# Encoder layer on one core: the value products of a head are issued one query tile later, and the read-back of its deviations is postponed

## The chip, the cores and the metric

The program runs on one core of a Trainium2 chip. The metric is device time in microseconds (us). TensorE (PE) does the matrix products, VectorE (DVE) and ScalarE (ACT) read the results out of the accumulators, GpSimd (POOL) helps, and SyncE (SP) issues almost all transfers. Each engine works through its own instructions in the order of the program; semaphores make one wait for another.

## The reference, cut to what matters

Two request groups of 1024 rows pass through one encoder layer with shared weights:

```python
proj = x @ w_in                          # x: layer norm of the input
s = einsum('bqhcd,bkhcd->bhcqk', q, k) * scale      # 4 heads, 2 maps (c) each
p = softmax(s); a = p[:, :, 0] - lam * p[:, :, 1]
o = einsum('bhqk,bkhd->bqhd', a, v)                 # "value products"
o_da = rms_norm(o, subln_g) * (1 - lam_init) * silu(g)
o_mx = cross-attention of 4 heads into 256 memory rows, times silu(g)
o_cv = gated width-3 convolution
x = layer_norm(alpha * x + concat(o_da, o_cv, o_mx) @ w_o)
```

Everything is float32. Each large product is done as three products of a high and a low half (hi x hi, hi x lo, lo x hi).

## The kernel before

The attention is cut into 20 jobs, numbered 0 to 19 here: for each group, the four heads with two halves of 512 query rows each, then two memory jobs (numbers 8, 9, 18 and 19). A job has four tiles. In tile s, `score` issues the scores of 128 query rows against all keys (12 matmuls into two accumulator tiles `ps` of the pool `psS`, which has two buffers), then the two row maxima `mx` on DVE (L633), two exponentials `e` on ACT (L634), and, when the planner's clock says so, the combination of the two maps on DVE (L639 to L642). `turn` (L677) transposes two key blocks of the job before into a `pt`, which takes a buffer of the same pool `psS`; ACT copies it to `th` (L690), and DVE makes the low half `tl` (L155). `av` (L695) issues the six value products into the accumulator `po` (its third product of a block, L714, reads `tl`; in memory jobs there are four products, L707 and L708). After the fourth `av` of a head, `end_head` squares `po` on ACT (L737) and multiplies it by gain and gate on DVE (L739, output `og`).

Between these steps stand the "passes": three matmuls each (L389 to L391) of the projection tiles, later of the output projection (L872). A projection tile of 512 columns takes 8 passes. `job_steps` writes a job as 20 steps, five to a tile, and `run` issues the job's passes in equal shares after each step. Before, the five steps of a tile are: scores; nothing; `turn` of the job before; nothing; `av` of the job before. So there are two shares of passes from scores to `turn`, two from `turn` to `av`, and one from `av` to the next scores. A written plan gives each job its passes: 48 for jobs 1, 2, 4, 13 and 15, 64 for 3 and 5, 56 for 6, 40 for 7, 8, 9, 16 and 17, and 32 for 0, 10, 11, 12, 14, 18 and 19. After job 19 a last loop runs its `turn` and `av` between passes of the output projection.

A planner's clock `fl.t` (ns) counts TensorE work only: 650 for a pass, 1400 for scores, 880 for a `turn`, 1380 for an `av`. `after(ns, fn)` emits `fn` into the engine's program that much later on this clock. A list `extra` holds small steps on TensorE with due times, which `run_extra` emits after passes: the turning of value tiles (accumulator `pvt`), the sum of a head's squares (`rms`, accumulator `pr`, L745) and the turning of its deviations (`rows`, accumulator `pw`). All three use the one buffer of `psX`. After `rows`, the deviations `rw` are written to DRAM (`rd`), read back spread over the partitions (`rb`, L768), and multiplied into `og` on POOL (`fin`, L771), which is then stored.

Buffers that matter: `sq`, `rw`, `rb` and the memory jobs' `bot` share one buffer (tag "sq"); `og` has two, `th` and `tl` one each, `po` one, "ev" (projection read-outs and loads) five. In jobs 7 and 8 `norm_rows` normalises the second group's input: loads `xt`, DVE (L291), POOL (L295, L152), DVE (L155).

Of the kernel before, what the change touches and what calls it, by code (L numbers as in the profile page):

```python
# [27 lines left out]
F32 = mybir.dt.float32  # L28
F32R = mybir.dt.float32r
AF = mybir.ActivationFunctionType  # L30
ALU = mybir.AluOpType
# [4 lines left out]
P = 128  # L36
D = 1024
S = 1024
HS = 512
KB = D // P  # L40
H = 4
DH = 64
# [23 lines left out]
FD = 800  # L66
RD = 2500
MD = 800

SETS = (("Q", 4), ("K", 4), ("V", 4), ("G", 4), ("CB", 2), ("CC", 2), ("CH", 2), ("CG", 2),  # L70
        ("QM", 2), ("GM", 2), ("MK", 2), ("MV", 2))
# [23 lines left out]
class Flow:  # L95
# [10 lines left out]
    def after(self, ns, fn):  # L106

        done = []

        def once():  # L110
            if not done:
                done.append(True)
                fn()
        self.n += 1
        heapq.heappush(self.due, (self.t + ns, self.n, once))
        return once
# [8 lines left out]
def encoder(ctx, tc, x0, x1, xt0, xt1, memt, wt, wo, cols, lam4, rope, ln_rows, y0, y1):  # L125
    nc = tc.nc
    X, XT, Y = (x0, x1), (xt0, xt1), (y0, y1)
    fl = Flow()
    after = fl.after
# [11 lines left out]
    def sb(shape, dt, tag, name):  # L141
        return pool.tile(shape, dt, tag=tag, name=name, bufs=BUFS.get(tag, 1))

    def bank(shape, name):

        return psX.tile(shape, F32, tag="x", name=name)

    dma = nc.sync.dma_start
    V, G, A, T = nc.vector, nc.gpsimd, nc.scalar, nc.tensor
# [4 lines left out]
    def lo_of(out, x, hi, eng=None):  # L154
        (eng or V).tensor_tensor(out, x, hi.bitcast(F32), op=ALU.subtract)  # L155
# [97 lines left out]
    def keep_stats(g):  # L253

        def turn():
            pw = bank([16, P], "pst")
            T.transpose(pw, stats[g].rearrange("p i t -> p (i t)"), const["ident"])
            rw = sb([16, P], F32, "sq", "strw")
            A.activation(rw, pw, AF.Copy)
            fl.pe(110)  # L260
            after(800, lambda: dma(st_d[g].rearrange("i (t c) -> (i t) c", c=P), rw))
        extra.append((fl.t, turn))
# [149 lines left out]
    def store(dst, src, ns=1500):  # L412
        after(ns, lambda: dma(dst, src))
# [147 lines left out]
    EVAC = dict(Q=evac_q, K=evac_k, V=evac_v, G=evac_gate(g_d), CB=evac_cb, CC=evac_cc, CH=evac_ch,  # L561
                CG=evac_cg, QM=evac_qm, GM=evac_gate(gm_d), MK=evac_mk, MV=evac_mv)

    extra = []

    def run_extra():

        while extra:
            due = min(extra, key=lambda x: x[0])
            if due[0] > fl.t:  # L570
                return
            extra.remove(due)
            due[1]()


    class Job:
# [70 lines left out]
        def score_mem(self, qt):  # L647
# [18 lines left out]
            def norm(h):  # L666
                if h == 0:
                    V.reciprocal(r, sm)  # L668
                s = slice(h * NMEM, (h + 1) * NMEM)
                G.tensor_scalar(e[:, s], e[:, s], r[:, h:h + 1], 1.0, op0=ALU.mult, op1=ALU.mult)  # L670
            for h in range(H):
                self.late.append(after(3000 + MD * h, lambda h=h: norm(h)))
            self.tiles.append(e)
# [3 lines left out]
        def turn(self, s):  # L677
            while self.late:
                self.late.pop(0)()
            b = 2 * (MEMORDER[s] if self.mem else s)  # L680
            pt = psS.tile([P, S], F32, tag="s", name="pt")
            for u in range(2):
                for i in range(4):
                    T.transpose(pt[:, u * HS + i * P:u * HS + (i + 1) * P],  # L684
                                self.tiles[i][:, (b + u) * P:(b + u + 1) * P], const["ident"])
            th = sb([P, S], F32R, "th", "th")
            tl = sb([P, S], F32R, "tl", "tl")

            def halves():
                A.activation(th, pt, AF.Copy)  # L690
                self.t = th, tl, after(1200, lambda: lo_of(tl, pt, th))
            self.t = th, tl, after(400, halves)
            fl.pe(880)

# [25 lines left out]

        def end_mem(self, h):
            po, p, r0 = self.po, h // 2, (h % 2) * DH
            bot = sb([DH, HS], F32, "sq", "bot")
            A.activation(bot, po[DH:P, :], AF.Copy)
            if h % 2 == 0:
                self.og = sb([P, HS], F32, "og", "ogm")
            og = self.og
            V.tensor_tensor(og[r0:r0 + DH, :], po[0:DH, :], bot, op=ALU.add)
            if h % 2 == 1:
                gt = self.gt[p]  # L730
                V.scalar_tensor_tensor(og, og, 0.5, gt, op0=ALU.mult, op1=ALU.mult)
                store(mix_d[self.g][self.half][6 + p], og)
# [9 lines left out]
        def rms(self):  # L742
            pr = bank([P, 4], "pr")
            for i in range(4):
                T.matmul(pr[:, i:i + 1], self.sq[:, i * P:(i + 1) * P], const["ones"], start=True, stop=True)  # L745
            ms, r0 = sb([P, 4], F32, "small", "ms"), self.r0
            V.scalar_tensor_tensor(ms, pr, 1.0 / P, r0, op0=ALU.mult, op1=ALU.mult)
            rs = sb([P, 4], F32, "small", "rs")
            G.tensor_tensor(ms, ms, r0, op=ALU.mult)
            G.tensor_scalar(ms, ms, 1.0, EPS, op0=ALU.mult, op1=ALU.add)  # L750
            G.tensor_tensor(ms, ms, const["mhalf"][:, 0:4], op=ALU.pow)
            G.tensor_tensor(rs, ms, r0, op=ALU.mult)
            g, h, half, og = self.g, self.h, self.half, self.og
            rd = dram.tile([4, P], F32, name=f"rd{g}_{h}_{half}")

            def rows():

                pw = bank([4, P], "pw")
                T.transpose(pw, rs, const["ident"])
                rw = sb([4, P], F32, "sq", "rw")  # L760
                V.tensor_copy(rw, pw)
                fl.pe(110)
                after(1500, lambda: dma(rd, rw))
                after(5000, lambda: spread())

                def spread():
                    self.rb = sb([P, HS], F32, "sq", "rb")
                    dma(self.rb, flat(rd, 0, [[0, P], [1, HS]]))  # L768

                def fin():  # L770
                    G.tensor_tensor(og, og, self.rb, op=ALU.mult)  # L771
                    store(mix_d[g][half][h], og)
                after(9500, fin)
            extra.append((fl.t + 6000, rows))
            fl.pe(100)

    def job_steps(job, prev, nxt):

        out = []
        memory = nxt and nxt.mem and not job.mem  # L780
        for s in range(4):
            out.append([lambda s=s: job.score(s)])
            out.append([])
            if prev:
                out.append([lambda s=s: prev.turn(s)])
                out.append([])
                out.append([lambda s=s: prev.av(s)])
            if prev and s == (0 if prev.mem else 1):
                out[-1].append(prev.load_gates)
            if s == 1:  # L790
                if memory:
                    out[-1].append(nxt.load_memory)
            if s == 2 and memory:
                out[-1].append(nxt.split_memory)
            if s == 3 and nxt and nxt.mem and job.mem:
                out[-1].append(lambda: (setattr(nxt, "k", job.k), setattr(nxt, "v", job.v)))
        return out

    def run(steps, until):

        total = fillers.left() - sum(KB for it in fillers.items[until:] if it[0] != "do")
        done = 0
        for n, step in enumerate(steps):
            for fn in step:
                fn()
            while done < total * (n + 1) // len(steps):
                fillers.step()
                done += 1
                run_extra()
# [115 lines left out]
    until = []  # L925
# [39 lines left out]
    jobs = [Job(g, h, half) for g in range(2) for h in (0, 1, 2, 3, None) for half in range(2)]  # L965
# [41 lines left out]
    while fillers.i < n_first:  # L1007
        fillers.step()
        run_extra()
        while early and early[0][0] <= fl.t:  # L1010
            early.pop(0)[1]()
    prev = None
    for n, job in enumerate(jobs):
        if n == 19:
            load_wo(0, W0)
        if n < 2:
            for i in range(4):
                after(1000 + 8000 * i, lambda t=4 * n + i: stats_step(t))
        if n in (7, 8):
            new_hT(n - 7)  # L1020
            norm_rows(1, n - 7, 3300, *(("cu", "cy") if n == 8 else ("cy", "cu")), (X1, X2, X3))
        run(job_steps(job, prev, jobs[n + 1] if n + 1 < len(jobs) else None), until[n])
        prev = job
    for s in range(4):
        if s == 0:
            prev.load_gates()
        prev.turn(s)
        for k in range(6):
            fillers.step()
            run_extra()  # L1030
        prev.av(s)
        for k in range(3):
            fillers.step()
            run_extra()
    while not fillers.done():
        fillers.step()
    fl.flush()
# [32 lines left out]
```

## Time and profile before

| | us |
|---|---|
| median of 3 runs (1322.15 to 1327.23) | 1324.88 |
| the profiled execution | 1324.38 |
| its span, first to last instruction | 1322.6 |
| PE busy | 1204.0 (91%) |
| DVE busy | 874.6 (66%) |
| POOL busy | 466.3 (35%) |
| ACT busy | 426.4 (32%) |

The mean granted TensorE clock is 0.969 of full speed. A matmul's busy time overlaps that of the next one, so PE's busy share is read together with its waits: 100% busy means only that no gap is longer than the overlap.

### The profile page before, as it was taken

Reading aid. Unit: us, or ns where it says so; the run is one execution under the profiler, and the core shown is the slowest. Engines: PE = TensorE matmul, PEld = TensorE weight load, DVE = VectorE, ACT = ScalarE, POOL = GpSimd, SP = SyncE. Lnnn points to the kernel's source line nnn. Section 1 sums busy time; section 2 is a strip of 40 time slices with the busy share of each in tenths; the row PEclk is TensorE's granted clock in tenths of the full one; section 3 lists DMA queues with packets and bytes.
Section 4 is the critical chain, followed back from the end, with each engine's and each line's share of the span. In section 5 each row is a group of like instructions: output and inputs, shape, how many; then the busy total and the mean of one; then the engine's idle time right before and its main releaser. Section 6 shows DMA issues by size and latency. Waiting matters only on the chain.

```text
span 1322.6 us, 15444 instructions
## 1 busy us (share of the span) xinstructions
PE 1204.0 (91%) x5850; PEld 930.8 (70%) x5850; DVE 874.6 (66%) x1211; ACT 426.4 (32%) x707; POOL 466.3 (35%) x500
## 2 busy tenths in 40 slices
PE   6779799999999997779988989999999999899997
PEld 4557567777777785657756667767777777688886
DVE  5688856574566567774766666656656657787776
ACT  3333233233323243233433332432323344221110
POOL 4544411141033325484511113313312236544443
PEclk8889999999999998988999999999999999899999
DMA  7514122111111333332301011021122136635441
GB/s 282 183 41 136 48 72 72 49 56 48 56 57 32 96 115 125 104 97 78 113 24 48 17 57 43 30 79 50 33 72 72 33 126 208 207 121 174 143 143 48
DMA packets 62138, 118.64 MB, mean 90 GB/s; under 512 B 5264, under 2 KB 23920, under 8 KB 61936
## 3 DMA queue, kind: packets, MB, share of 16 engines
q1 hardware_dynamic: 58608, 111.36, 25.4%
q10 hardware_dynamic: 3456, 6.29, 1.2%
q8 instruction: 46, 0.75, 0.2%
q14 instruction: 28, 0.23, 0.1%
HBM read 93.47 MB, written 24.17 MB: 89 GB/s over the span
## 4 chain that ended last, share of the span: by engine, by line
PE 56%; DVE 20%; ACT 7%; POOL 7%; issue 5%; DMA 3%; SPq 1%; POOLq 0%; DVEq 0%; ACTq 0%
PE pout L872 10%; PE ps L626 7%; ACT e L634 4%; DVE tl L155 3%; DVE mx L633 3%; PE po L714 3%; PE pt L684 3%; DVE e L642 2%; PE pV L389 2%; PE pV L390 2%; PE pV L391 2%; PE po L713 2%; PE po L712 2%; DVE wl L155 1%; PE pQ L389 1%
## 5 line engine op out<-in xcount | busy, mean ns | idle before, releaser
L634 ACT ACTIVATE e<-ps,mx 128x1024 f32<-128x1024 f32 x128 | 142.9, 1116 | 345.4 <-DVE mx L633 345.4
L633 DVE TENSOR_REDUCE mx<-ps 128x1 f32<-128x1024 f32 x128 | 150.6, 1218 | 94.7 <-PE ps L626 94.5
L152 POOL TENSOR_SCALAR wh<-wraw 128x1024 fp32r<-128x1024 f32 (+1 forms) x73 | 76.2, 1044 | 245.6 <-PE pCC L390 54.6
L155 DVE TENSOR_TENSOR wl<-wraw,wh 128x1024 fp32r<-128x1024 f32 (+1 forms) x72 | 95.6, 1328 | 32.1 <-POOL wh L152 25.3
L155 DVE TENSOR_TENSOR tl<-pt,th 128x1024 fp32r<-128x1024 f32 x80 | 97.4, 1217 | 11.5 <-ACT th L690 11.0
L872 PE MATMUL pout<-woh,mixh 128*128 128x512 f32 x256 | 101.9, 398 | 0.0
L872 PE MATMUL pout<-woh,mixl 128*128 128x512 f32 x256 | 101.1, 395 | 0.1
L872 PE MATMUL pout<-wol,mixh 128*128 128x512 f32 x256 | 100.4, 392 | 0.0
L690 ACT ACTIVATE th<-pt 128x1024 fp32r<-128x1024 f32 x80 | 82.1, 1027 | 50.6 <-PE pt L684 49.9
L714 PE MATMUL po<-tl,vh 128*128 128x512 f32 x128 | 56.6, 442 | 42.8 <-DVE tl L155 42.4
L642 DVE SCALAR_TENSOR_TENSOR e<-e,ssum,e 128x1024 f32<-128x1024 f32 x64 | 89.1, 1392 | 0.0
L427 POOL TENSOR_TENSOR sw<-sw,ropet 128x512 f32<-128x512 f32 x32 | 41.8, 1306 | 115.0 <-DVE sw L421 115.0
L864 POOL TENSOR_TENSOR xr<-xr,lnrow 128x512 f32<-128x512 f32 x32 | 54.5, 1721 | 67.4 <-DVE xr L861 67.4
L684 PE MATMUL pt<-ident,e 128*128 128x128 f32 x512 | 68.9, 279 | 8.3 <-ACT e L634 8.2
L684 PEld LDWEIGHTS pt<-ident,e 128*128 128x128 f32 x512 | 60.2, 144 | 21.0 <-ACT e L634 14.6
L714 PEld LDWEIGHTS po<-tl,vh 128*128 128x128 f32 x128 | 25.2, 197 | 62.0 <-DVE tl L155 57.3
L626 PE MATMUL ps<-kh,qh 64*128 64x512 f32 x256 | 58.1, 450 | 0.0
L389 PE MATMUL pK<-hTh,wh 128*128 128x512 f32 x128 | 53.4, 417 | 4.6 <-ACT hTh L299 3.2
L872 PEld LDWEIGHTS pout<-woh,mixl 128*128 128x128 f32 x256 | 48.5, 189 | 11.7 <-DVE mixl L155 0.5
L872 PEld LDWEIGHTS pout<-wol,mixh 128*128 128x128 f32 x256 | 48.5, 190 | 10.6
L872 PEld LDWEIGHTS pout<-woh,mixh 128*128 128x128 f32 x256 | 48.6, 190 | 9.9
L670 POOL TENSOR_SCALAR em<-em,rm 128x256 f32<-128x256 f32 x64 | 35.8, 571 | 54.7 <-DVE rm L668 50.5
(227 smaller groups left out, 3121.9 us busy)
## 6 DMA issues: line engine op xcount, KB each, us to landing
wraw<-in_wt SPq DMA_DIRECT2D x73, 512.0 KB, 3.6
mraw<-mix SPq DMA_DIRECT2D x16, 512.0 KB, 6.2
xr<-in_x SPq DMA_DIRECT2D x16, 512.0 KB, 6.1
out<-xr ACTq DMA_DIRECT2D x24, 256.0 KB, 2.0
x<-in_x SPq DMA_DIRECT2D x8, 512.0 KB, 9.1
gate<-gs SPq DMA_DIRECT2D x16, 256.0 KB, 2.1
xs<-in_x SPq DMA_DIRECT2D x8, 512.0 KB, 5.8
gt<-gate SPq DMA_DIRECT2D x16, 256.0 KB, 4.2
```

Source lines behind the costliest of these rows:

```text
L152: G.tensor_scalar(out, x, scale, 1.0, op0=ALU.mult, op1=ALU.mult)
L155: (eng or V).tensor_tensor(out, x, hi.bitcast(F32), op=ALU.subtract)
L389: T.matmul(ps, wh[:, k], hh, start=kb == 0, stop=False)
L626: T.matmul(ps[c][:, n], q[r, qt * P:(qt + 1) * P], k[r, n], start=i == 0, stop=i == 2)
L633: V.tensor_reduce(mx[:, c:c + 1], ps[c], AX.X, ALU.max, negate=True)
L634: A.activation(e[c], ps[c], AF.Exp, bias=mx[:, c:c + 1], accum_out=sm[:, c:c + 1])
L642: V.scalar_tensor_tensor(e[0], e[1], st, e[0], op0=ALU.mult, op1=ALU.add)
L684: T.transpose(pt[:, u * HS + i * P:u * HS + (i + 1) * P], self.tiles[i][:, (b + u) * P:(b + u + 1) * P], const["ident"])
L690: A.activation(th, pt, AF.Copy)
L714: T.matmul(self.po, vh[:, k, :], tl[:, c], start=False, stop=end)
L864: after(2200 + 2000 * n, lambda c=c: G.tensor_tensor(xt[:, c], xt[:, c], ab[:, c], op=ALU.add))
L872: T.matmul(self.ps, a[:, kb, :], b, start=kb == 0 and ti == 0, stop=kb == KB - 1 and ti == 2)
```

## The change

`av` of tile s moves from the last step of tile s to the first step of tile s+1, behind the next tile's scores; the fourth `av` of a job is issued behind the first scores of the job after next (`prev2`). The steps of a tile are now: scores and `av`; `turn`; nothing; nothing; nothing. The low half `tl` is posted 1800 instead of 1200 on the planner's clock. `run_extra` leaves at least `XB` = 2600 between two small steps. The write of a head's deviations is posted 2500 instead of 1500 after `rows`, their read-back 12000 instead of 5000, the multiplication 17000 instead of 9500. In memory jobs the copy `bot` goes into the rows of `og` that it is added to, and no longer into the shared "sq" buffer; the turned statistics `strw` use an "ev" buffer. The gates of a head are loaded in the step of the scores.

```diff
+XB = 2600
-            rw = sb([16, P], F32, "sq", "strw")
+            rw = sb([16, P], F32, "ev", "strw")
-    extra = []
+    extra, busy = [], [0.0]
     def run_extra():
         while extra:
             due = min(extra, key=lambda x: x[0])
-            if due[0] > fl.t:
+            if due[0] > fl.t or busy[0] > fl.t:
                 return
             extra.remove(due)
             due[1]()
+            busy[0] = fl.t + XB
-                self.t = th, tl, after(1200, lambda: lo_of(tl, pt, th))
+                self.t = th, tl, after(1800, lambda: lo_of(tl, pt, th))
         def end_mem(self, h):
-            bot = sb([DH, HS], F32, "sq", "bot")
-            A.activation(bot, po[DH:P, :], AF.Copy)
             if h % 2 == 0:
                 self.og = sb([P, HS], F32, "og", "ogm")
-            V.tensor_tensor(og[r0:r0 + DH, :], po[0:DH, :], bot, op=ALU.add)
+            A.activation(og[r0:r0 + DH, :], po[DH:P, :], AF.Copy)
+            V.tensor_tensor(og[r0:r0 + DH, :], po[0:DH, :], og[r0:r0 + DH, :], op=ALU.add)
-                after(1500, lambda: dma(rd, rw))
-                after(5000, lambda: spread())
+                after(2500, lambda: dma(rd, rw))
+                after(12000, lambda: spread())
-                after(9500, fin)
+                after(17000, fin)
-    def job_steps(job, prev, nxt):
+    def job_steps(job, prev, prev2, nxt):
         for s in range(4):
             out.append([lambda s=s: job.score(s)])
-            out.append([])
-            if prev:
-                out.append([lambda s=s: prev.turn(s)])
-                out.append([])
-                out.append([lambda s=s: prev.av(s)])
+            if s == 0 and prev2:
+                out[-1].append(lambda: prev2.av(3))
+            if s and prev:
+                out[-1].append(lambda s=s: prev.av(s - 1))
             if prev and s == (0 if prev.mem else 1):
                 out[-1].append(prev.load_gates)
+            out.append([lambda s=s: prev.turn(s)] if prev else [])
+            out += [[], []]
...
+            out.append([])
     for s in range(4):
+        prev.av(s - 1) if s else prev2.av(3)
         if s == 0:
             prev.load_gates()
-        prev.turn(s)
-        for k in range(6):
+        for k in range(2):
             fillers.step()
             run_extra()
-        prev.av(s)
-        for k in range(3):
+        prev.turn(s)
+        for k in range(7):
             fillers.step()
             run_extra()
+    prev.av(3)
```

## Rows read from the trace of the kernel before

**Rows 1.** What PE waited for, whole span: us in total, times, longest us.

```profile
PE po L714 <- DVE tl L155: 42.4, 26, 6.6
PE po L708 <- DVE tl L155: 15.5, 10, 3.4
PE pt L684 <- ACT e L634: 9.5, 16, 2.1
PE pr L745 <- ACT vt L457: 8.7, 4, 2.2
```

**Rows 2.** Busy time by job (1, 2, 3, 4, 6): stretch, length, engines, clock, DMA.

```profile
132.70:196.00 63.30, 53.26 (x260) 40.29 (x259) 43.32 (x80) 18.55 (x30) 20.00 (x24) 0.97 0.19 63
196.00:246.60 50.60, 50.53 (x260) 39.60 (x259) 31.50 (x43) 15.85 (x24) 7.23 (x12) 1.00 0.18 58
246.60:308.20 61.60, 61.60 (x310) 49.01 (x309) 37.85 (x55) 18.99 (x29) 20.50 (x21) 1.00 0.18 56
308.20:363.30 55.10, 52.85 (x264) 41.38 (x263) 28.34 (x38) 17.55 (x27) 7.53 (x11) 0.97 0.17 53
424.90:485.80 60.90, 58.37 (x286) 45.65 (x285) 34.51 (x44) 18.64 (x29) 16.32 (x16) 0.97 0.24 72
```

**Rows 3.** The same view of jobs 10, 11, 12, 13, 14 and 16.

```profile
653.40:703.50 50.10, 41.33 (x197) 29.61 (x196) 34.61 (x51) 18.53 (x29) 10.65 (x10) 0.94 0.13 43
703.50:750.10 46.60, 41.14 (x205) 29.94 (x204) 28.72 (x40) 16.91 (x26) 7.64 (x8) 0.99 0.14 46
750.10:797.10 47.00, 42.60 (x210) 31.05 (x209) 29.03 (x41) 14.88 (x22) 6.07 (x11) 0.96 0.12 40
797.10:849.70 52.60, 51.01 (x264) 39.94 (x263) 36.65 (x53) 17.23 (x27) 19.63 (x18) 1.00 0.14 46
849.70:897.40 47.70, 41.83 (x214) 30.59 (x213) 26.85 (x37) 17.17 (x26) 7.68 (x9) 1.00 0.17 56
...
949.90:1001.50 51.60, 47.87 (x238) 36.67 (x237) 29.55 (x39) 17.32 (x27) 8.94 (x11) 0.97 0.19 56
```

**Rows 4.** Timeline of the second tile of job 11: start, us, engine, instruction.

```profile
715.92 0.50 PE L626 MATMUL ps<-kh,qh 64*128 64x512 f32 x2
720.12 1.09 PE L684 MATMUL pt<-ident,e 128*128 128x128 f32 x8 [0.26 <-ACT e L634]
724.88 0.50 PE L714 MATMUL po<-tl,vh 128*128 128x512 f32 x1 [1.13 <-DVE tl L155]
...
717.61 2.35 DVE L633 TENSOR_REDUCE mx<-ps 128x1 f32<-128x1024 f32 x2 [0.27 <-PE ps L626]
721.29 0.17 DVE L639 RECIPROCAL r<-sm 128x2 f32<-128x2 f32 x1 [1.33 <-ACT e L634]
723.61 1.22 DVE L155 TENSOR_TENSOR tl<-pt,th 128x1024 fp32r<-128x1024 f32 x1
```

**Rows 5.** What PE waited for in the stretch of jobs 7 and 8.

```profile
PE po L714 <- DVE tl L155: 20.3, 6, 6.6
PE po L712 <- ACT th L690: 3.2, 2, 1.9
```

**Rows 6.** Jobs 7 and 8: busy time as in rows 2.

```profile
485.80:551.40 65.60, 49.59 (x236) 37.40 (x235) 50.67 (x59) 22.74 (x35) 31.62 (x30) 0.92 0.40 134
551.40:610.90 59.50, 48.53 (x238) 36.47 (x237) 39.79 (x47) 20.81 (x51) 43.65 (x46) 0.90 0.27 89
```

**Rows 7.** Timeline of DVE in job 7.

```profile
510.93 0.75 DVE L291 SCALAR_TENSOR_TENSOR xt<-xt,ccol,strow 128x512 f32<-128x512 f32 x1 [4.87 <-DMA xt<-in_xt]
```

**Rows 8.** What PE waited for in the stretch of job 19 and the last loop.

```profile
PE po L708 <- DVE tl L155: 7.1, 5, 3.4
```

**Rows 9.** What DVE, POOL and SP's queue waited for, whole span.

```profile
DVE og L739 <- ACT sq L737: 36.4, 16, 4.1
POOL og L771 <- DMA rb<-rd: 19.2, 4, 11.7
SPq L768 <- DMA rd<-rw: 13.1, 13, 3.1
```

More of the change, by code (lines that the diff above doesn't have):

```diff
@@ L782, in job_steps @@
             out.append([lambda s=s: job.score(s)])
-            out.append([])
-            if prev:
-                out.append([lambda s=s: prev.turn(s)])
-                out.append([])
-                out.append([lambda s=s: prev.av(s)])
+            if s == 0 and prev2:
+                out[-1].append(lambda: prev2.av(3))
+            if s and prev:
+                out[-1].append(lambda s=s: prev.av(s - 1))
             if prev and s == (0 if prev.mem else 1):
                 out[-1].append(prev.load_gates)
-            if s == 1:
-                if memory:
-                    out[-1].append(nxt.load_memory)
+            out.append([lambda s=s: prev.turn(s)] if prev else [])
+            out += [[], []]
+            if s == 1 and memory:
+                out[-1].append(nxt.load_memory)
+            out.append([])
             if s == 2 and memory:
@@ L1011, in encoder @@
             early.pop(0)[1]()
-    prev = None
+    prev = prev2 = None
     for n, job in enumerate(jobs):
@@ L1021, in encoder @@
             norm_rows(1, n - 7, 3300, *(("cu", "cy") if n == 8 else ("cy", "cu")), (X1, X2, X3))
-        run(job_steps(job, prev, jobs[n + 1] if n + 1 < len(jobs) else None), until[n])
-        prev = job
+        run(job_steps(job, prev, prev2, jobs[n + 1] if n + 1 < len(jobs) else None), until[n])
+        prev, prev2 = job, prev
     for s in range(4):
+        prev.av(s - 1) if s else prev2.av(3)
         if s == 0:
             prev.load_gates()
-        prev.turn(s)
-        for k in range(6):
+        for k in range(2):
             fillers.step()
             run_extra()
-        prev.av(s)
-        for k in range(3):
+        prev.turn(s)
+        for k in range(7):
             fillers.step()
             run_extra()
+    prev.av(3)
     while not fillers.done():
```

## The prediction, before the result was known

> **What bounds the kernel now.** I read the page first: PE is busy for 91% of the span, DVE for 66%, ACT and POOL for a third, so TensorE is the bound, and what can be won is its waiting time and its half-speed time. Second, the list of what PE waited for [rows 1]. The reader is to see that two lines, the third value product waiting for the low half `tl`, hold 57.9 us (42.4 + 15.5), while the transposes waiting for `e` hold 9.5 and the squares waiting for the value turn's accumulator 8.7.
>
> Third, busy time cut at each job's first scores [rows 2, 3]. Job 2 takes 50.6 us with 48 passes and job 3 61.6 us with 64, both with PE busy throughout and the clock at 1.00. So a pass costs (61.6 - 50.6) / 16 = 0.69 us, and the attention of a job 50.6 - 48 x 0.69 = 17.6 us. A job without waits would take 39.6 us with 32 passes, 45.1 with 40, 50.6 with 48 and 56.1 with 56. Against that, the jobs with 32 passes (10, 11, 12, 14) took 50.1, 46.6, 47.0 and 47.7 us, an excess of 33.0 together; jobs with 48 or 64 passes have little or none, except job 1.
>
> Fourth, one tile of job 11 in order of time, which says why [rows 4]. Scores start at 715.92, the maxima at 717.61, the combination of the maps can start only at 721.29, after both exponentials, and `tl` ends at 723.61 + 1.22 = 724.83. PE, which has two shares of 1.6 passes (2.2 us) between the end of the transposes (721.2) and the products, arrives early and stands 1.13 us. With 48 passes two shares are 3.3 us, which is just enough: that is why the long jobs do not wait. The chain scores, maxima, exponentials, combination, `tl` takes 8.9 us from the start of the scores; the old order adds products and one more share behind it before the next scores.
>
> **The change, part by part.** (1) *The products move behind the next scores.* No matmul is added or removed. PE no longer meets `tl` at the products but at the next scores, which need the accumulator buffer that `tl` reads. Between the transposes and that point stand four shares instead of two. In a 32-pass job the cycle scores to `tl` is 8.9 us and an unhindered tile 39.6 / 4 = 9.9, so it fits with 1 us to spare; other DVE work, moved between by the later posting of `tl` (1800 for 1200 in the planner's time, under one pass), can eat that. I leave 2 us per job for it and 3 more in job 10, where each tile also ends a memory head. Jobs 10, 11, 12 and 14: 33.0 - 8 - 3 = 22 us won (bounds 0 and 33).
>
> (2) *Small steps kept 2600 apart.* The squares waited 2.2 us for the value turn's read-out, four times [rows 1]; four passes (2.8 us) now cover it. Jobs 4, 6 and 16 exceed their bare times by 4.5, 4.8 and 6.5 [rows 2, 3], 15.8 in all: the 2.2 each, about (1 - 0.97) x 55 = 1.7 each of half clock, and in job 16 some waits for `tl`. Keeping 1 us each as remainder, 12.8 won (bounds 6 and 15.8).
>
> (3) *Job 13*, and 15 like it, exceeds 50.6 by 2.0 [rows 3]: 3 won of the two. *Job 1* exceeds it by 12.7 [rows 2]. The wait for `tl` there gets two more shares (3.3 us) of cover; I take 5 (bounds 0 and 10).
>
> (4) *Jobs 7 and 8* exceed 45.1 by 20.5 and 14.4, and wait 23.5 us for `th` and `tl` in eight places [rows 5, 6]. Four more passes (2.8 us) of cover each would take at most 8 x 2.8 = 22 us. But here DVE itself is late: it stood 4.87 us for a load of `xt` ahead of the combination and `tl` [rows 7], and POOL is busy for 43.65 of 59.5 us in job 8. What DVE loses there stays lost for the next maxima. I take 10, nearer to the lower bound of 0 than to 22.
>
> (5) *Job 19 and the last loop* wait 7.1 us for `tl` [rows 8]. In job 19 that goes; in the loop only one pass more (0.7 us) is gained per tile. 4 won (bounds 1 and 7).
>
> (6) *Read-back later.* The SP queue stood 13.1 us in thirteen waits for the write of `rd`, and POOL 19.2 us in four for `rb` [rows 9]. Both go, since the read-back is 9.5 us of planner's time behind the write. Each head still issues the same two small transfers, one POOL product and one store; moved later, they pass other weight loads in the SP queue, which gain by it. PE waited for none of them, so I count 0. The covers: the last head's store leaves during job 19's end, and the output rows that read it come after eight others.
>
> (7) *Buffers.* "sq" is now held from `end_head` until POOL has read `rb`: 5000 + 6000 + 17000 = 28.0 us of planner's time and up to two spacings of 2.6, so 33.3; the shortest head job lasts 4 x 8.86 = 35.4 by that clock. It fits, barely. `og` is held as long: in jobs 9 and 19 the memory head's second `og` may find it still in use and hold ACT for some us, covered by four shares: I take 1 us (bounds 0 and 6). The gate loads of memory jobs now come right after the fourth product that still uses the buffer, so SP waits for DVE there, in three places; weights are loaded two tiles ahead, so 0. `bot` and `strw`: the same instructions in other buffers, 0.
>
> (8) *What it costs.* Before the transposes PE now has six products (1.4 us) and one share instead of two shares: 2.5 us against 2.2 with 32 passes, but 3.0 against 3.3 with 48. No wait for `e` is listed in jobs 2 to 6, so I charge 2 us for eight long jobs (bounds 0 and 9.6, that is 0.3 x 32 tiles).
>
> The sum: 22 + 12.8 + 3 + 5 + 10 + 4 - 1 - 2 = 54 us. The profiled execution took 1324.4 us, 0.5 under the median of the three runs; 1324.4 - 54 = 1270.
>
> **The rivals.** *DVE is held behind ACT.* At a head's end DVE multiplies `po` only after ACT has squared it: 36.4 us of DVE waiting in 16 places, 2.3 each [rows 9]. Now the square stands on ACT behind both exponentials of the scores just issued. By [rows 4] DVE is free at 717.61 + 2.35 = 719.96, the exponentials end by 721.29, the square 0.6 later: 1.9 us of DVE standing still at the time when it used to make weight halves, before combination and `tl`. If PE waited for all of it in all 16 heads, 30 us of the 54 would go: 1300. For: it lies in the cycle that is 1 us short of bounding. Against: it was 2.3 before, and the long jobs have over 3 us of cover. The Trainium skill, PSUM — Partial Sum Buffer, section on bank collisions, bears on this: any two engines' accesses to one accumulator bank and quadrant have to be kept apart, reads too, so the multiplication can't be let past the square. This trace agrees: each of the 16 multiplications waited for its square.
>
> *The clock stays low.* Part of the time TensorE is granted 1.2 instead of 2.4 GHz after it stood idle. Clocks of 0.94 in job 10, 0.96 in 12 and 0.97 in 4, 6 and 16 [rows 2, 3] cost 3.0 + 1.9 + 1.7 + 1.8 + 1.5 = 10 us; if short remaining waits kept those stretches, the gain is 44: 1280. Against: job 14 held 1.00 in spite of its waits. The Trainium skill, TensorE: Matmul & The Clock Gate, section on psum-queue depth-cycling, says that frequent short idles between groups of matmuls can make the clock swing; job 14's row does not show it.
>
> *Jobs 7 and 8 come free.* If the eight waits there were only a matter of order, all 35 us of excess might go instead of 10: 1245. Against: the `xt` loads and POOL's load.
>
> *Nothing moves.* If `tl` is late because DVE is full, the same wait appears at the next scores and the time stays, within 7 us. For: DVE is the releaser in both lines. Against: DVE is busy 28.7 of 46.6 us in job 11 [rows 3].
>
> *Slower: the "sq" buffer.* If the read-back slips past the 35.4 us of (7), the next head's square waits on ACT for `rb` to be released, and the next exponentials queue behind it. It decides when the slip exceeds what is left, 2 us of planner's time; to undo 54 us it must hold each of 16 heads over 3.4 us, and with 5 us each the time is 1324.4 - 54 + 80 = 1350. Against: in jobs with 48 passes the margin is over 10 us.
>
> **How the numbers follow.** The forecast (1254 to 1288) has 0.52, the clock case 0.06, DVE held (1288 to 1317) 0.20, jobs 7 and 8 free 0.10, nothing 0.06, slower 0.06. The predicted time is that of the likeliest, 1270. From 1244 to 1310 leaves out the two last cases, a tail of the third and one of the fourth, under 0.2. Half a per cent, about what a measurement of this kernel can tell from no change, is 6.6 us: faster 0.88, same 0.06, slower 0.06.
>
> **What would show it.** In the new profile the lines for L714 and L708 waiting for `tl` should be almost gone, and scores (L626) waiting for `tl` should appear with under 15 us; the squares' wait of 8.7 should be near 0; jobs 10, 11, 12 and 14 should take 41 to 43 us each, jobs 2, 3 and 5 the same as before within 1; jobs 7 and 8 should keep most of their excess; SP's wait for `rd` and POOL's for `rb` should be gone. I am wrong if the waits for `e` at the transposes grow past 15 us, if scores wait for `tl` by as much as the products did, or if ACT waits for POOL before a square.

## The result, and the profile after

The changed kernel takes 1282.88 us (median of 4 runs, 1282.34 to 1283.52) against 1324.31 for the kernel before, run beside it (4 runs): ratio 0.9686, 95% interval 0.9666 to 0.9706, about 41 us faster. The forecast was 54 (1270), its range 1244 to 1310. The profiled execution took 1283.52, its span is 1281.7, PE is busy for 1191.1 of it (93%, before 91%), and the clock is 0.971. Lines of `kernel.py` stand one or two lower than before: scores are L628, the transposes L686, third products L716 and L710, halves L156, the end of a memory head L728 to L732.

What PE waited for, whole span of the changed kernel (us in total, times, longest):

```profile
PE pt L686 <- ACT e L636: 18.2, 17, 4.2
PE ps L628 <- DVE tl L156: 17.0, 8, 5.9
...
PE po L710 <- DVE tl L156: 5.3, 5, 1.6
...
PE pout L875 <- ACT mixh L856: 4.0, 1, 4.0
...
PE po L716 <- DVE tl L156: 3.4, 1, 3.4
...
PE pout L875 <- DVE mixl L156: 2.9, 1, 2.9
```

The 57.9 us of products waiting for `tl` [rows 1] are 8.7 (5.3 + 3.4), and the squares' line is gone. Five lines are new or longer: scores wait 17.0 us for `tl`, transposes 18.2 for `e` (9.5 before), the output projection 6.9 for its input (two lines), and one turning of a value tile, in job 8, 3.6 for its own. Cut to jobs 7, 10 and 11, the scores' line shows 9.2, 5.6 and 1.9 of its 17.0; the rest of the span has next to none.

Busy time by job of the changed kernel, columns as in rows 2: jobs 1, 2, 4, then 7, 8, then 10, 11, 12, 14, then 16, and from job 19 to the end:

```profile
131.00:187.80 56.80, 51.70 (x254) 40.55 (x253) 42.90 (x80) 18.07 (x29) 21.66 (x24) 0.94 0.20 70
187.80:239.20 51.40, 50.19 (x260) 39.55 (x259) 32.40 (x43) 15.80 (x24) 7.38 (x12) 1.00 0.18 57
300.80:351.20 50.40, 50.40 (x262) 40.02 (x261) 29.48 (x38) 17.55 (x27) 6.85 (x11) 1.00 0.20 58
...
469.80:536.10 66.30, 52.10 (x234) 39.35 (x233) 49.05 (x59) 22.74 (x35) 31.84 (x30) 0.90 0.38 124
536.10:589.90 53.80, 46.06 (x240) 36.30 (x239) 37.20 (x44) 20.84 (x51) 43.52 (x42) 0.94 0.28 90
...
630.90:679.60 48.70, 41.93 (x197) 31.41 (x196) 35.98 (x52) 19.28 (x30) 14.23 (x14) 0.93 0.14 49
679.60:723.20 43.60, 40.97 (x205) 31.17 (x204) 29.55 (x42) 17.01 (x26) 7.88 (x8) 0.96 0.13 43
723.20:764.40 41.20, 40.32 (x212) 30.54 (x211) 28.92 (x40) 14.68 (x22) 6.15 (x11) 1.00 0.13 46
816.50:858.10 41.60, 40.83 (x216) 31.00 (x215) 27.19 (x37) 16.96 (x26) 6.84 (x9) 1.00 0.19 64
910.30:955.30 45.00, 45.00 (x239) 35.51 (x238) 30.94 (x39) 17.34 (x27) 8.73 (x11) 1.00 0.17 53
1036.90:1281.70 244.80, 224.29 (x1024) 180.84 (x1023) 179.35 (x231) 58.46 (x85) 118.58 (x108) 0.97 0.44 150
```

Against [rows 2, 3, 6], in the order of the forecast's sum (us won between the two profiled executions; jobs 6 and 13 went from 60.9 to 56.9 and from 52.6 to 52.1, job 15 from 52.5 to 52.2, the last stretch from 237.7 to 244.8):

| step | forecast | measured |
|---|---|---|
| (1) jobs 10, 11, 12, 14 | 22 | 1.4 + 3.0 + 5.8 + 6.1 = 16.3 |
| (2) jobs 4, 6, 16 | 12.8 | 4.7 + 4.0 + 6.6 = 15.3 |
| (3) jobs 13 and 15 | 3 | 0.8 |
| (3) job 1 | 5 | 6.5 |
| (4) jobs 7 and 8 | 10 | -0.7 + 5.7 = 5.0 |
| (5) job 19 and the last loop | 4 | -7.1 |
| everything else, (7) and (8) with it | -3 | 4 |

Two places stand out in the changed kernel. The first is the end of a memory head, here in the first tile of job 11, on DVE:

```profile
681.33 2.35 DVE L635 TENSOR_REDUCE mx<-ps 128x1 f32<-128x1024 f32 x2 [1.59 <-PE ps L628]
685.64 0.68 DVE L729 TENSOR_TENSOR ogm<-po,ogm 64x512 f32<-64x512 f32 x1 [1.95 <-ACT ogm L728]
...
687.40 1.21 DVE L156 TENSOR_TENSOR wl<-wraw,wh 128x1024 fp32r<-128x1024 f32 x1
688.53 0.15 DVE L641 RECIPROCAL r<-sm 128x2 f32<-128x2 f32 x1
...
690.83 1.22 DVE L156 TENSOR_TENSOR tl<-pt,th 128x1024 fp32r<-128x1024 f32 x1
```

From the start of the maxima to the end of `tl` is 10.72 us; in [rows 4], a tile with no such end, it was 7.22. When the maxima are done, DVE stands 1.95 us until ACT, which has the two exponentials of the new scores in front, has copied the lower half of `po`; then the gate and a weight half come, and the combination starts 7.20 us after the start of the maxima.

The second is SP's queue in the last loop, where one entry, the load of the gates, lasts 11.15 us; behind it stand the loads of the output projection and the store of the last head:

```profile
1070.20 11.15 SPq L613 DMA_DIRECT2D gt<-gm  x2
1081.45 0.85 SPq L837 DMA_DIRECT2D lnrow<-in_ln_rows  x2
1082.39 0.38 SPq L849 DMA_DIRECT2D mraw<-mix  x1
...
1084.53 1.10 SPq L414 DMA_DIRECT2D mix<-og  x1
```

What DVE, POOL and SP's queue waited for, whole span; the first three lines answer to rows 9, the last two are new:

```profile
DVE og L740 <- ACT sq L738: 30.6, 16, 2.5
POOL og L772 <- DMA rb<-rd: 2.0, 1, 2.0
SPq L769 <- DMA rd<-rw: 7.6, 5, 3.6
DVE ogm L729 <- ACT ogm L728: 21.7, 12, 2.6
SPq L613 <- DVE ogm L732: 27.7, 2, 17.4
```

### The profile page after: what moved, and what is told of

Read it like the earlier page. It is cut to its first block, busy times and chain, and to the rows that moved or that the text cites. A ratio compares the mean times of both kernels' runs of the same rounds, so it can differ in the third digit from the quotient of the medians.

```text
span 1281.7 us, 15455 instructions
## 1 busy us (share of the span) xinstructions
PE 1191.1 (93%) x5850; PEld 932.5 (73%) x5850; DVE 876.8 (68%) x1211; ACT 425.2 (33%) x707; POOL 472.5 (37%) x500
## 5 line engine op out<-in xcount | busy, mean ns | idle before, releaser
L156 DVE TENSOR_TENSOR wl<-wraw,wh 128x1024 fp32r<-128x1024 f32 (+1 forms) x72 | 101.5, 1409 | 35.6 <-POOL wh L153 29.7
L156 DVE TENSOR_TENSOR tl<-pt,th 128x1024 fp32r<-128x1024 f32 x80 | 97.2, 1215 | 1.0 <-ACT th L692 0.8
L644 DVE SCALAR_TENSOR_TENSOR e<-e,ssum,e 128x1024 f32<-128x1024 f32 x64 | 86.2, 1347 | 0.0
L686 PE MATMUL pt<-ident,e 128*128 128x128 f32 x512 | 68.4, 277 | 17.3 <-ACT e L636 17.1
L628 PE MATMUL ps<-kh,qh 64*128 64x512 f32 x256 | 67.3, 453 | 17.0 <-DVE tl L156 17.0
L686 PEld LDWEIGHTS pt<-ident,e 128*128 128x128 f32 x512 | 58.7, 142 | 31.5 <-ACT e L636 26.1
L672 POOL TENSOR_SCALAR em<-em,rm 128x256 f32<-128x256 f32 x64 | 46.9, 746 | 49.5 <-DVE rm L670 30.5
L628 PEld LDWEIGHTS ps<-kh,qh 64*128 64x128 f32 x256 | 29.4, 187 | 45.2 <-DVE tl L156 19.8
L628 PE MATMUL ps<-kl,qh 64*128 64x512 f32 x256 | 59.6, 406 | 1.6 <-DVE kl L431 1.6
L875 PEld LDWEIGHTS pout<-woh,mixh 128*128 128x128 f32 x256 | 48.5, 189 | 15.1 <-ACT mixh L856 4.4
L714 PE MATMUL po<-th,vh 128*128 128x512 f32 x128 | 58.8, 459 | 0.0
L628 PE MATMUL ps<-kh,ql 64*128 64x512 f32 x256 | 58.7, 403 | 0.0
```

The source lines that it names most:

```text
L628: T.matmul(ps[c][:, n], q[r, qt * P:(qt + 1) * P], k[r, n], start=i == 0, stop=i == 2)
L644: V.scalar_tensor_tensor(e[0], e[1], st, e[0], op0=ALU.mult, op1=ALU.add)
L686: T.transpose(pt[:, u * HS + i * P:u * HS + (i + 1) * P], self.tiles[i][:, (b + u) * P:(b + u + 1) * P], const["ident"])
L714: T.matmul(self.po, vh[:, k, :], th[:, c], start=k == 0, stop=False)
L875: T.matmul(self.ps, a[:, kb, :], b, start=kb == 0 and ti == 0, stop=kb == KB - 1 and ti == 2)
```

## The experiments

All edits are made to the changed kernel unless another base is named. Each kernel computes the whole layer. After each median stands the ratio to the kernel before, run beside it (its medians are 1322.2 to 1322.8), with the 95% interval; the change itself is 0.9686 [0.9666, 0.9706]. A thousandth is 1.3 us.

**The last stretch: output buffer or gate loads?** (7) had named both, with 1 us and with nothing. First the last head's `og` is given back early:

```diff
-                after(12000, lambda: spread())
-                after(17000, fin)
+                late = (12000, 17000) if (h, half) != (3, 1) else (4500, 7500)
+                after(late[0], lambda: spread())
+                after(late[1], fin)
```

> The changed kernel, but the last head of each group (the one ahead of the memory jobs) has its deviations read back at 4500 and multiplied at 7500 on the planner's clock instead of 12000 and 17000. Theory (the memory head's second og waits for the last head's store: ACT stood 11.69 us there, and the output product for mixh and mixl behind it): that wait falls under 3 us, PE's waits for mixh and mixl (4.0 and 2.9) go, and the time falls by 5 to 9 us, to 1274 to 1278. Rival (the last loop is late because the gate loads hold the SP queue for 10.3 us, whoever holds og): ACT's wait shrinks but PE's waits for mixh and mixl stay, and the time is within 2 us of 1283.

Measured: 1282.96 us, 0.9695 [0.9678, 0.9713], no difference. ACT's wait for `og` at the memory head is gone and the last stretch stays within 1.4 us of what it was, and so does SP's wait for the gates' buffer, in this kernel:

```profile
SPq L613 <- DVE ogm L732: 28.5, 2, 20.7
...
1037.30:1280.70 243.40, 224.58 (x1024) 181.78 (x1023) 178.27 (x231) 58.55 (x85) 118.31 (x108) 0.97 0.44 150
```

So giving `og` back early wins nothing by itself: PE's 4.0 us of waiting for `mixh` are gone, but it then waits 5.2 us for `mixl` instead of 2.9. Then the gates of the memory jobs are loaded one tile later, when their buffer is free:

```diff
-            if prev and s == (0 if prev.mem else 1):
+            if prev and s == 1:
                 out[-1].append(prev.load_gates)
...
-        if s == 0:
+        if s == 1:
             prev.load_gates()
```

> The changed kernel with the gates of the memory jobs loaded in the second tile of the next job (and of the last loop) instead of the first, where SP has to wait for DVE's last use of the buffer. Theory (the last loop got 7 us longer because the gate loads hold the SP queue, so that the output's loads come late): SP's wait at the gates (28.2 us in two) falls under 10, PE's waits for mixh and mixl (4.0 and 2.9) go, the stretch from job 19's first scores to the end falls from 236.7 to about 231, and the time by 4 to 8 us. Rival (the last loop is longer because DVE is late there, whatever SP does): SP's wait falls, the stretch stays within 2 us and so does the time.

Measured: 1274.76 us, 0.9644 [0.9626, 0.9663], some 5.6 us better than the change; the intervals just clear each other. In its trace SP waits for no gate, the `mraw` load that followed the gates is issued 40.2 us after job 19's start (45.5 in the changed kernel: 1082.39 - 1036.90), and the last stretch is back to 238.3 (before the change 237.7):

```profile
1074.90 1.94 SPq L849 DMA_DIRECT2D mraw<-mix  x1
...
1034.70:1273.00 238.30, 222.04 (x1024) 180.34 (x1023) 179.46 (x231) 58.61 (x85) 118.41 (x108) 0.99 0.45 154
```

So the loss of the last stretch comes from the gate load at the head of SP's queue. The hold itself isn't new, for in the kernel before SP stood almost as long:

```profile
1111.91 0.32 SPq L413 DMA_DIRECT2D mix<-og  x1
...
1114.33 9.59 SPq L611 DMA_DIRECT2D gt<-gm  x2
```

But there it was over 39.0 us after job 19's start (now 44.5), and the last head's store left ahead of it, not behind. ACT's wait for that store, 11.7 us in the changed kernel and none before, falls to 5.3 with the gates later. SP's longer hold at a gate, 17.4 us in job 11, costs nothing that shows: jobs 10 and 11 take 92.3 us with it and without.

**Jobs 10 and 11: DVE behind ACT.** The DVE part of a head's end is posted 2600 later, so that DVE has other work while ACT gets to `po` (the same in `end_head`):

```diff
...
+            def close():
+                V.tensor_tensor(og[r0:r0 + DH, :], po[0:DH, :], og[r0:r0 + DH, :], op=ALU.add)
+                if h % 2 == 1:
+                    V.scalar_tensor_tensor(og, og, 0.5, gt, op0=ALU.mult, op1=ALU.mult)
+                    store(dst, og)
+            after(2600, close)
```

> The changed kernel with the DVE part of a head's end (gain and gate, and the memory head's addition) posted 2600 later on the planner's clock, so that DVE is not held behind ACT's square or copy. Theory (DVE held behind ACT 1.9 us per head end makes tl late in jobs 10 and 11): DVE's waits for sq and ogm (30.6 and 21.7 us) fall under 10, the scores' wait for tl falls by 3 to 5 us, job 10 shortens by 3 to 6 us, and the time falls by 3 to 7. Rival (the work only moves on DVE and tl comes no earlier, since the same instructions still stand ahead of it): DVE's waits fall but the time stays within 2 us.

Measured: 1270.96 us, 0.9604 [0.9589, 0.9619], 11 us better. Its waits, its jobs 10 and 11, and DVE in the same first tile of job 11:

```profile
PE ps L628 <- DVE tl L156: 9.2, 5, 6.2
...
DVE ogm L732 <- ACT ogm L728: 2.3, 4, 0.8
...
624.90:668.80 43.90, 39.11 (x197) 29.01 (x196) 36.22 (x52) 18.64 (x29) 12.59 (x12) 1.00 0.16 54
668.80:709.10 40.30, 39.40 (x205) 29.74 (x204) 28.98 (x41) 17.00 (x26) 8.28 (x8) 1.00 0.15 47
...
670.52 2.35 DVE L635 TENSOR_REDUCE mx<-ps 128x1 f32<-128x1024 f32 x2 [2.19 <-PE ps L628]
672.79 1.22 DVE L156 TENSOR_TENSOR wl<-wraw,wh 128x1024 fp32r<-128x1024 f32 x1
674.20 0.17 DVE L641 RECIPROCAL r<-sm 128x2 f32<-128x2 f32 x1 [0.20 <-ACT e L636]
...
677.96 1.22 DVE L156 TENSOR_TENSOR tl<-pt,th 128x1024 fp32r<-128x1024 f32 x1
```

The weight half now fills the time in which DVE stood still, the combination starts 3.68 us after the maxima instead of 7.20, and `tl` ends after 8.66 instead of 10.72. Jobs 10 and 11 go from 92.3 to 84.2 us, 8.1 of the 11. By the rows 3.7 of these are PE's idle time and 4.4 its busy time: its clock there rises from 0.93 and 0.96 to 1.00. Another 3.0 are job 1 (53.8), which takes 54.9 to 57.6 in the other kernels of this order, 56.4 in one that has this edit too; so they aren't counted for it.

**`tl` earlier.** It is posted at 600 instead of 1800.

```diff
-                self.t = th, tl, after(1800, lambda: lo_of(tl, pt, th))
+                self.t = th, tl, after(600, lambda: lo_of(tl, pt, th))
```

> The changed kernel with tl posted 600 instead of 1800 after th on the planner's clock, so that it stands ahead of more of DVE's other work. Theory (in jobs 7 and 8 tl is late because loads' consumers and weight halves stand ahead of it): the scores' wait for tl (17.0 us) falls under 11 and the time by 4 to 8 us. Rival (tl in front then itself waits for th on ACT and holds DVE, as before the change): DVE's wait of tl for th rises from 0.8 us to over 8, and the time is within 2 us or higher.

Measured: 1277.13 us, 0.9654 [0.964, 0.9668]. Its waits:

```profile
PE pt L686 <- ACT e L636: 25.3, 23, 3.9
...
PE ps L628 <- DVE tl L156: 6.1, 2, 4.8
```

The scores' wait falls by 10.9, the transposes' wait for `e` rises by 7.1: other DVE work is done later for it, the next maxima among it (in one tile of job 7 they start 5.9 us after the scores instead of 3.6), and most of the saving is paid at the transposes. Some 4 us better by the ratio, with intervals that touch. The gain came from jobs 10 and 11 (87.1 together against 92.3) and some 3 us of the last stretch; job 7 took 68.4 and gained nothing, so the theory had the wrong place. The rival's sign did not come: DVE's wait of `tl` for `th` rose only to 3.5 us.

**Job 7: the loads of `xt`.** In the changed kernel DVE still stands for `xt` ahead of `tl` [rows 7], and scores wait 5.9 us behind it:

```profile
496.92 0.75 DVE L292 SCALAR_TENSOR_TENSOR xt<-xt,ccol,strow 128x512 f32<-128x512 f32 x1 [4.24 <-DMA xt<-in_xt]
...
501.95 1.22 DVE L156 TENSOR_TENSOR tl<-pt,th 128x1024 fp32r<-128x1024 f32 x1
```

The DVE steps on `xt` are posted 2500 later:

```diff
-X1, X2, X3 = 3000, 4200, 6200
+X1, X2, X3 = 5500, 6700, 8700
```

> The changed kernel with the second group's normalisation in jobs 7 and 8 posted 2500 later behind its loads (5500, 6700, 8700 for 3000, 4200, 6200). Theory (DVE stands in front of loads of xt, 5.8 us in two places, and tl queues behind): those waits go, the scores' wait for tl in job 7 (10 us in three tiles) falls by half, job 7 shortens from 66 to about 60 us, and the time falls by 4 to 8. Rival (the loads themselves are late, since their buffers come free later now, or POOL is the bound there): DVE waits elsewhere, and jobs 7 and 8 together stay within 3 us of 120.

Measured: 1278.03 us, 0.9662 [0.9644, 0.968], some 3 us better by the ratio, but the intervals overlap; what is shown is the place. DVE's wait for `xt` fell from 5.8 to 0.4 us over the span, the scores' wait in job 7 from 9.2 to 3.1, and job 7 from 66.3 to 60.1 (63.3 to 68.4 in the kernels with the new order and the old times of `xt`), of which job 9 gives 1.6 back:

```profile
468.60:528.70 60.10, 51.40 (x236) 39.23 (x235) 48.83 (x59) 22.74 (x35) 31.47 (x30) 0.89 0.42 138
```

**The spacing, taken out and alone.** First out of the changed kernel:

```diff
-XB = 2600
+XB = 0
```

> The changed kernel without the spacing of the small steps (XB = 0). Theory (the spacing is what removed the squares' wait for the value turn, with the half clock behind it): the waits of pr for vt come back, two to four of about 2.2 us, jobs 4, 6, 14 or 16 lengthen by about 4 each, and the time rises by 8 to 14 us. Rival (the new order alone moved the squares away from the value turns, since a head now ends behind the next job's first scores): no such wait and a time within 2 us of 1283.

Measured: 1283.38 us, 0.9705 [0.9685, 0.9724], no difference; no line of squares waiting for the value turn's read-out came back, and jobs 4, 6 and 16 took 50.4, 56.9 and 45.0 as in the changed kernel. The theory fell. Then the other way round, the kernel before with the spacing alone (and `strw` in an "ev" buffer):

```diff
+XB = 2600
...
-            rw = sb([16, P], F32, "sq", "strw")
+            rw = sb([16, P], F32, "ev", "strw")
...
-    extra = []
+    extra, busy = [], [0.0]
...
-            if due[0] > fl.t:
+            if due[0] > fl.t or busy[0] > fl.t:
                 return
...
+            busy[0] = fl.t + XB
```

> The kernel before with the spacing of the small steps alone (XB = 2600, and the statistics' copy in an ev buffer), products where they were. Theory (in the old order the squares meet the value turn, and the spacing parts them; in the new order the move does it): PE's waits of pr for vt (8.7 us) fall under 2 and the time falls by 8 to 15 us against the kernel before. Rival (the spacing does nothing in either order): the waits stay and the time is within 3 us of the kernel before.

Measured: 1308.35 us, 0.9886 [0.9866, 0.9906], some 15 us better than the kernel before. Jobs 4, 6, 14 and 16 took 51.0, 57.0, 44.4 and 47.7 (55.1, 60.9, 47.7 and 51.6 before), and the squares' line is gone, while the waits for `tl` stayed:

```profile
PE po L716 <- DVE tl L156: 41.4, 26, 6.6
PE po L710 <- DVE tl L156: 16.6, 10, 3.6
```

So the spacing is worth about 15 us in the old order and nothing in the new one.

**The read-back at its old times.**

```diff
-                after(2500, lambda: dma(rd, rw))
-                after(12000, lambda: spread())
-                after(17000, fin)
+                after(1500, lambda: dma(rd, rw))
+                after(5000, lambda: spread())
+                after(9500, fin)
```

> The changed kernel with the read-back of all heads at the old times (1500, 5000, 9500). Theory (the later read-back wins nothing on PE and costs the wait of ACT in the last loop): the waits of SP for rd (13.1 us) and of POOL for rb (19.2 us) come back about as before, PE does not wait for either, and the time falls as in the run with the last heads alone, by 5 to 9 us. Rival (the waits of SP and POOL cost PE something in the new order, where weights and keys are tighter): the time is 1283 or more, at least 5 us above the run with the last heads alone.

Measured: 1276.47 us, 0.9647 [0.9632, 0.9662], 5 us better by the ratio; the interval just clears that of the change. Only 1.1 us of it has a place that repeats, job 2 (job 7 took 63.3, which is within its variation):

```profile
186.90:237.20 50.30, 50.18 (x260) 39.54 (x259) 31.33 (x43) 15.80 (x24) 7.40 (x12) 1.00 0.18 58
...
225.02 1.23 DVE L156 TENSOR_TENSOR wl<-wraw,wh 128x1024 fp32r<-128x1024 f32 x1 [2.33 <-POOL wh L153]
```

**The move alone.** The changed kernel without its spacing, with the old read-back and with `tl` at 1200 as before:

```diff
-XB = 2600
+XB = 0
-                self.t = th, tl, after(1800, lambda: lo_of(tl, pt, th))
+                self.t = th, tl, after(1200, lambda: lo_of(tl, pt, th))
...
+                after(1500, lambda: dma(rd, rw))
+                after(5000, lambda: spread())
+                after(9500, fin)
```

> The move of the products alone: the changed kernel without the spacing (XB = 0), with the read-back at the old times and tl at 1200. Theory (the whole gain is the move, the rest of the change costs): no wait of pr for vt, the scores' wait for tl as in the changed kernel, and 1273 to 1279, that is 4 to 10 us less than the change as it was made. Rival (spacing and read-back each look free alone only because the other covers for it): 1283 or more.

Measured: 1278.64 us, 0.9672 [0.9653, 0.969]. The intervals overlap: the move (with the buffers and the gates' new place that go with it) gives the whole gain, and the three other edits together give nothing that can be measured, nor do they cost anything that can, as the theory had it. With `tl` at 1200 the scores wait 7.6 us for it instead of 17.0, the transposes 20.7 for `e` instead of 18.2.

**The cures together.** The later head's end, gates and `xt` in one kernel:

```diff
-X1, X2, X3 = 3000, 4200, 6200
+X1, X2, X3 = 5500, 6700, 8700
...
+            after(2600, close)
...
-        if s == 0:
+        if s == 1:
             prev.load_gates()
```

> The changed kernel with three of the single edits together: DVE's part of a head's end posted 2600 later, the memory jobs' gates one tile later, and the normalisation in jobs 7 and 8 posted 2500 later. Theory (three separate places: jobs 1, 10 and 11; the last loop; job 7): the single gains of 12, 8 and 5 us add up, the time is 1256 to 1261. Rival (a common part, such as DVE's lateness, was counted more than once): the time is above 1264.

Measured: 1257.06 us, 0.950 [0.948, 0.952], some 25 us under the change; no other kernel here has a lower median. One by one they gave 10.8 + 5.6 + 3.2 = 19.6 by their ratios, so they don't get in each other's way. Its waits at transposes and scores:

```profile
PE pt L686 <- ACT e L636: 19.8, 19, 3.7
...
PE ps L628 <- DVE tl L156: 4.6, 5, 1.8
```

With the old read-back times in addition:

```diff
...
-                after(17000, fin)
+                after(9500, fin)
```

> As the run with three edits, and the read-back at the old times too (1500, 5000, 9500). Theory (the later read-back costs some 6 us in the changed kernel, at places that the other three edits don't touch: jobs 2 and 7, and the last loop's og): 4 to 7 us less than with three edits, 1251 to 1256. Rival (its gain was the wait for og in the last loop and chance in job 7, which are gone with the other edits): within 2 us of the run with three edits.

Measured: 1257.78 us, 0.9518 [0.9501, 0.9534]. The 5 us of the old read-back don't appear again: the intervals of the two kernels overlap. And that kernel with `tl` at 600:

```diff
-                self.t = th, tl, after(1800, lambda: lo_of(tl, pt, th))
+                self.t = th, tl, after(600, lambda: lo_of(tl, pt, th))
```

> As the run with four edits, and tl posted 600 instead of 1800 later. Theory (its 6 us of gain alone came from jobs 10 and 11, where DVE's part of the head's end stood ahead of tl, and which the first edit has cured): within 2 us of the run with four edits. Rival (tl ahead of weight halves helps in its own right): 3 to 6 us less.

Measured: 1259.96 us, 0.9533 [0.9519, 0.9546], no gain: once DVE no longer stands behind ACT, an early `tl` only lengthens the transposes' wait for `e`, from 17.9 to 26.7 us in 22 places.

## Why the prediction was right, and where its sum was off

Direction and mechanism were right: the third products no longer meet `tl` (57.9 us became 8.7), and of the 40.9 us by which the span got shorter 28.0 are time in which PE stood idle. The other 12.9 are PE's busy time, which was not taken apart. The sum was 13 too high, and its terms were off in both directions. That it came no further off is partly luck: (2) came by another way, and the places that no term names gave 4 where 3 was charged, among them 1.7 ahead of job 0's first scores and 1.5 in job 9.

**(1), 16.3 of 22, mis-sized by the rival it had priced.** Jobs 12 and 14 came as forecast, 41.2 and 41.6 us within "41 to 43"; but one of the four squares' waits stood in job 14, and the spacing alone takes 3.3 off it, so some 3 of its 6.1 belong to (2). Jobs 10 and 11 took 48.7 and 43.6. A memory head ends in each tile of job 10 and, since the move, in the first of job 11, and there DVE stood 1.95 us behind ACT, the 1.9 that the rival "DVE is held behind ACT" had worked out. The prediction charged job 10 with only 3 us more than the others and did not see that its last head now ends in job 11; moving DVE's part later gave back 8.1 in the two, 4.4 of it as PE's busy time at the higher clock. The rival's other half was wrong: in the long jobs DVE waits for the square as it did (30.6 us in 16 places), and jobs 3 (61.6), 5 and 16 lost nothing to it.

**(2), 15.3 of 12.8, the right size with the wrong cause.** The step that failed is "Small steps kept 2600 apart". Without the spacing the same jobs take the same time. The spacing does what the text says in the old order (jobs 4, 6 and 16 get 11.9 us shorter by it), but the move alone also parts the squares from the value turns. That it does so because a head's end now comes behind the first scores of a later job is argued from the order, not tried.

**(3)** gave 0.8 of 3 and job 1 6.5 of 5, within its variation. **(4)** gave 5.0 of 10: jobs 7 and 8 kept 29.9 of their 34.9 us of excess, as "most of their excess" said, and job 7's loss was named in its place, DVE standing for `xt`; posting those steps later took 6.2 us off it. What POOL's 43.52 busy us of 53.80 do to job 8 was not tried.

**(5) and (7), -7.1 where 4 - 1 was expected: the one step with the wrong sign.** "SP waits for DVE there, in three places; weights are loaded two tiles ahead, so 0" asked only for the weights. In the last loop other things stand behind those loads: the `mraw` loads and the last stores of the output projection's input. The gates held SP 10.3 us there, later than before the change, and PE met it as 4.0 + 2.9 us of waiting for `mixh` and `mixl`. The `og` buffer, which (7) had down for 1 us, held ACT 11.7 us, but giving it back early won at most 1.4 us of the stretch; with the gates later 6.5 of the 7.1 came back.

**(6), counted at 0.** It has a cost of 1.1 us in job 2, where the late product on POOL lands beside a weight half on DVE (below); the 5 us of the single experiment were not found again on top of the three cures, so the rest stays open between 0 and 4. SP still waits for `rd`, 7.6 us in 5 places instead of 13.1 in 13, so "gone" was wrong for it; POOL's 19.2 for `rb` are 2.0.

**(8), charged 2 and read as the sign of being wrong past 15.** The transposes' wait for `e` went from 9.5 to 18.2. 10.1 of that sit in jobs 1 and 7; jobs 2 to 6, for which the charge was made, have 2.1. The scores' wait for `tl`, 17.0, also passed the 15 named for it. The range held all the same: both were set as sums over the span, when the waits sit in a few tiles of jobs 1, 7, 10 and 11. The next gain lay in the scores' line, from which the later head's end took 7.8. Why the transposes' wait grew stands in the trace. Its eight waits over 0.8 us (15.1 of 18.2, in jobs 1, 2, 6, 7, 13 and 15) come behind maxima that DVE started 1.3 to 3.6 us after the last matmul of the scores (0.03 us in most tiles), and each time DVE had worked without a pause on other things: weight halves, low halves of keys and queries, the combination. The transposes need an accumulator buffer that the exponentials behind these maxima still read. So the step that failed is the charge by PE's cover alone, "2.5 us against 2.2" and "3.0 against 3.3"; how late DVE is was not in it. No kernel of this order brought the wait under 15.4 us.

The clock rival, "if short remaining waits kept those stretches", came in one of the five stretches that it named: job 10 is at 0.93 (0.94 before), while jobs 4, 6, 12 and 16, at 0.96 and 0.97 before, are granted 1.00, with short waits left in job 12. But the mean is 0.971 as against 0.969, since the clock fell elsewhere, in job 1 from 0.97 to 0.94 and in job 11 from 0.99 to 0.96. So of its 10 us only job 10's 3.0 came, and that the time, 1283, lies nearer to its 1280 than to 1270 does not make it right. "Slower by the sq buffer" did not come either: ACT waits for POOL before no square.

## What to carry to other kernels

When an instruction moves, look at what it now stands behind and what stands behind it in every queue that works in order, and ask of all that follows, not only of what you know to be loaded early: an entry that waits for its buffer delayed transfers that had nothing to do with it. A wait taken from one consumer turns up at the next with less cover, so price the new meeting place tile by tile, above all in tiles with one more duty than the rest. Two cures of one wait don't add: test each part in the order before and in the order after.

## What the hardware showed that was not expected

In job 2 of the changed kernel a weight half on DVE took nearly twice its usual time. These are POOL, DVE and PE there:

```profile
225.85 1.30 POOL L772 TENSOR_TENSOR og<-og,rb 128x512 f32<-128x512 f32 x1
...
225.93 2.31 DVE L156 TENSOR_TENSOR wl<-wraw,wh 128x1024 fp32r<-128x1024 f32 x1 [2.34 <-POOL wh L153]
...
231.32 1.09 PE L686 MATMUL pt<-ident,e 128*128 128x128 f32 x8 [1.21 <-ACT e L636]
```

With the old read-back times the product falls elsewhere, and the same instruction takes 1.23 us (above). Job 2 takes 50.3 or 50.4 us in all four kernels with the old times and the new order, and 51.4 in the others of that order. The 1.08 us more are about what was left of POOL's 1.30 when DVE started (1.22). PE met it at the transposes (the last line): the maxima and the exponentials came later by it, and in the kernel with the old times PE waits nowhere in job 2. The Trainium skill, SBUF — State Buffer, section "SBUF: two separate sides", says that VectorE and GpSimd share a pair of ports as an exclusive lock: of a GpSimd operation and a VectorE one with two operands in SBUF, where the GpSimd one reads there too, whichever starts first has the pair to its end, and the other is held up. The trace agrees: 1.23 us became 2.31.

It is not this place alone. Of the changed kernel's 65 such weight halves 20 take 1.44 to 2.31 us, and each of the 20 began while a POOL instruction ran; of the 45 others, 1.19 to 1.23 us, only two did. The 80 low halves `tl`, which DVE makes in instructions of the same size but with one operand in an accumulator, take 1.19 to 1.23 us, though POOL ran beside 31 of them. In the kernel before 12 weight halves were long. The late product lengthens a weight half to 2.3 us in jobs 3, 4 and 5 too, and there PE waits for nothing, so only job 2 pays for it.
